# Weight sums begun in the first attention; the second block's head products in plain order, rotary tables loaded wide, x rows' work pinned in program order

## The chip, the cores and the metric

One core of one Trainium2 chip runs the whole program in one launch. The metric is device microseconds of one execution. The kernel before takes 2484.66 us, the median of 3 runs (2481.41 to 2484.78).

## The reference

One layer of a decoder trunk over 2048 tokens of width 1024, all in float32: retention heads beside a pooling mixer behind one combined projection, then cross-attention to 256 memory tokens, then a gated feed-forward with a causal convolution. Cut to what matters:

```
proj = rmsnorm(x) @ w_in                       # 1024 -> 2560: q, k, v, gate (512 each), u (512)
y_ret = silu(g) * head_rmsnorm(retention(rope(q), rope(k), v))     # 4 heads of 128, chunks of 128
y_pool = pool_mixer(u)                         # 4 groups of 128, trailing windows 2, 4, 8, 16
x = x + concat(y_ret, y_pool) @ w_out
s = (rmsnorm(x) @ wq) @ k_mem^T / 16           # 4 heads of 256, 256 memory tokens
x = x + (softmax(s) @ v_mem) @ wo
a = rmsnorm(x) @ w_up                          # 1024 -> 2 * 2816
x = x + (silu(gate(conv3(a))) * val(conv3(a))) @ w_down
return rmsnorm(x)
```

## The kernel before

**Tiling.** The tokens are worked in two blocks b of 1024, each in two halves of 512. A tensor of 1024 x 1024 is eight row tiles k of 128 partitions. Every operand of a product is split into a high and a low part (`split`: ScalarE makes the high part, L258 or with a scale L261; VectorE subtracts it, L242 or L250), and every product is three matmuls, high by high, high by low, low by high (`passes`, L266 to L268), of 128 x 512 each.

**Stages in order of program.** Folding of the weights of memory and cross-attention; block 0: values, head inputs, retention and pooling, output projection with residual; `attention` of block 0; the product of its probabilities with the folded values (tables VWd, with the residual Xd loaded and stored, and the x rows of the next block loaded by `fetch_x`, L578, into T, and split by `load_x`, L261); block 1: `values` and beside it `quarter_sums`, then `head_projections`, output projection, attention, the same product; then the feed-forward over both blocks.

**`attention`** loads the folded memory tables from Md (`load_m`, L927: raw tiles R and S, split into Z at L258), makes the row statistics by small matmuls (L347) of a sum T which VectorE accumulates at L242, and then goes through 16 score tiles: a product, maximum, Exp (L969), division, and two tiles later a transposition (`turn`, L942 and L944).

**`head_projections`** (second block only) makes the sixteen head groups (q 0 to 3, k 4 to 7, gates 8 to 11, pooling groups 12 to 15) in eight pairs, `PAIRS`. For each pair seven products of half the size replace eight: sums of quarters of the weights (Ad, made ahead in DRAM; loaded into R at L1108 and split at L1114) against sums of quarters of x (made by `quarter_sums` and `turned_sums`). `Heads.evac` takes a product out of its accumulator, on ScalarE at L1691 when it is the first of its part, and `Heads.final` finishes a part: rotation for q and k (L1699, L1707), Silu for gates (L1718), negation for pooling groups, which then go through `pool_steps`, a list of VectorE steps. Products 0, 2, 4 and 6 of a pair stand behind one another in pairs 1 to 7 and 1, 3, 5 come after; the first pair has 0 to 6. `settle` splits a finished part for the output projection (E<-Z). Retention of a head (`kept`, L793 to L845) runs piece by piece between the products.

**`weight_sums`** makes the sums of weight quarters in DRAM, on POOL's queue (GpSimd), by DMAs that copy or accumulate: 42 jobs (8 for `PAIRS`, then the feed-forward's) of 8 DMAs in four steps. Each turn of its loop starts one job, and steps all that are live. A turn has a **tick**: a small copy on ScalarE that is kept in program order (L1027, halo<-consts), and behind it a copy on POOL (L1028), after which the DMAs of the turn are issued. Its holder `under[0]` is stepped by other loops, `spacing[0]` of their steps for one turn: by `units` in the output projection and the product after the attention when `slow[0]` is off, by each score tile i of the attention (from i = 2 on in block 0) and by each product of the heads.

**What sets the order.** The program is written as generators which are stepped beside each other. A scheduler that simulates time then moves instructions on each engine within their dependencies; those under `tc.keep_in_program_order` keep their written order among themselves, and `tc.issue_after` holds a DMA behind an instruction. Each engine then takes its instructions strictly in that order, so one that waits holds all behind it.

## Time and profile before

| | |
|---|---|
| median of 3 runs | 2484.66 us |
| the profiled execution's own time | 2485.51 us |
| its span in the trace | 2483.7 us |
| mean granted TensorE clock | 0.991 |
| TensorE busy | 2422.2 us (98%), 11294 matmuls |
| VectorE busy | 1731.1 us (70%) |
| ScalarE busy | 1289.8 us (52%) |
| GpSimd (POOL) busy | 318.8 us (13%) |
| moved by DMA | 501.56 MB |

Where the stages lie in that trace: the first block's output projection runs from about 370 us, its attention's tables are split up to 489, its scores begin at 491, the product of probabilities and values runs to about 664, the second block's values and quarter sums follow up to 705, the heads up to about 940, and the second attention takes in 1000 to 1060.

In the rows of the profile T, R, S, Z, Q, G, E are places in the on-chip memory, mm and aux are accumulators of TensorE, and names that end in d are in DRAM. The arrow in brackets at the end of a timeline row tells how long its engine had stood idle and what released it. "PEclk" is the granted clock of TensorE as a share of the full one. "DMA to landing" gives, for the loads of a line, the least, median and greatest time from issue to landing.

### The profile page before, as it was taken

The page shows a single profiled execution, that of the slowest core. Times are in us where ns is not written, and L with a number is a line of the kernel's source. Part 1 is how long each engine was busy: PE and PEld are TensorE (multiplying, and loading weights), DVE is VectorE, ACT ScalarE, POOL GpSimd, SP SyncE. Part 2 cuts the span into 40 slices and gives each one's busy share as a digit, 9 for nine tenths or more (in the row PEclk, how much of TensorE's full clock was granted, in tenths as well). Part 3 has the DMA queues.
Part 4 walks back from the last instruction along what each step waited for, and adds up shares of the span by engine and source line. Part 5 has one row for each costly group of instructions (what it writes and reads, how often), then busy time and mean ns, then how long its engine had stood idle before and what let it go on. Part 6 is the DMA issues. An engine that isn't in the chain of part 4 may idle for free.

```text
span 2483.7 us, 33285 instructions
## 1 busy us (share of the span) xinstructions
PE 2422.2 (98%) x11294; PEld 2020.2 (81%) x11294; DVE 1731.1 (70%) x2921; ACT 1289.8 (52%) x2348; POOL 318.8 (13%) x485
## 2 busy tenths in 40 slices
PE   6999999899999999999999999999999999999997
PEld 6888888788877787888888888888888888888886
DVE  8646566465665666575688776897667688867876
ACT  6333423343434554434555555665555677666663
POOL 1000003241155544000000000020000000000000
PEclk9999999999999999999999999999999999999998
DMA  8133528977599999557468655665456468768951
GB/s 290 46 108 111 162 73 237 279 173 234 171 296 257 262 235 278 159 175 253 153 187 276 215 187 169 211 219 172 162 157 216 132 223 305 244 189 267 353 173 68
DMA packets 263163, 501.56 MB, mean 202 GB/s; under 512 B 28752, under 2 KB 57552, under 8 KB 262992
## 3 DMA queue, kind: packets, MB, share of 16 engines
q1 hardware_dynamic: 201104, 385.11, 47.3%
q0 software_dynamic: 37376, 86.00, 14.9%
q10 hardware_dynamic: 24512, 28.32, 3.3%
q8 instruction: 89, 1.46, 0.2%
q14 instruction: 82, 0.67, 0.1%
HBM read 398.13 MB, written 187.17 MB: 236 GB/s over the span
## 4 chain that ended last, share of the span: by engine, by line
PE 91%; DMA 4%; DVE 3%; ACT 1%; issue 1%; SPq 0%; POOL 0%; POOLq 0%; ACTq 0%; DVEq 0%
PE mm L266 28%; PE mm L267 28%; PE mm L268 28%; DMA T<-Xd 1%; DMA Z<-xT 1%; PE aux L793 1%; PE aux L804 1%; DMA S<-Md 1%; PE aux L820 1%; PE aux L266 1%; PE aux L267 1%; PE aux L268 1%; DVE Z L242 1%; PE aux L822 1%; DVE T L242 0%
## 5 line engine op out<-in xcount | busy, mean ns | idle before, releaser
L266 PE MATMUL mm<-G,Q 128*128 128x512 f32 (+1 forms) x1745 | 673.6, 387 | 23.0 <-ACT Q L258 10.4
L268 PE MATMUL mm<-G,Q 128*128 128x512 f32 (+1 forms) x1745 | 669.7, 385 | 6.5 <-DVE Q L242 6.3
L267 PE MATMUL mm<-G,Q 128*128 128x512 f32 (+1 forms) x1617 | 620.1, 384 | 0.0
L267 PE MATMUL mm<-G,E 128*128 128x512 f32 x1084 | 421.6, 389 | 0.0
L266 PE MATMUL mm<-G,E 128*128 128x512 f32 x1084 | 420.1, 389 | 0.0
L268 PE MATMUL mm<-G,E 128*128 128x512 f32 x1084 | 419.2, 389 | 0.0
L266 PEld LDWEIGHTS mm<-G,Q 128*128 128x128 f32 x1745 | 331.5, 190 | 89.5 <-ACT Q L258 11.5
L268 PEld LDWEIGHTS mm<-G,Q 128*128 128x128 f32 x1745 | 330.9, 190 | 71.7 <-DVE Q L242 8.8
L267 PEld LDWEIGHTS mm<-G,Q 128*128 128x128 f32 x1617 | 307.5, 190 | 56.3
L242 DVE TENSOR_TENSOR Z<-Z,mm 128x512 f32<-128x512 f32 x296 | 201.8, 683 | 106.4 <-PE mm L268 106.1
L250 DVE SCALAR_TENSOR_TENSOR Z<-Z,vecs 128x1024 f32<-128x1024 f32 x176 | 224.7, 1280 | 50.0 <-ACT Z L1177 46.5
L268 PEld LDWEIGHTS mm<-G,E 128*128 128x128 f32 x1084 | 203.5, 188 | 42.4
L267 PEld LDWEIGHTS mm<-G,E 128*128 128x128 f32 x1084 | 203.5, 188 | 42.2
L266 PEld LDWEIGHTS mm<-G,E 128*128 128x128 f32 x1084 | 203.5, 188 | 42.2
L1114 ACT ACTIVATE E<-R 128x512 fp32r<-128x512 f32 (+1 forms) x165 | 101.5, 615 | 142.0 <-PE mm L267 134.1
L242 DVE TENSOR_TENSOR T<-T 128x512 f32<-128x512 f32 (+3 forms) x220 | 150.9, 689 | 24.2 <-ACT T L409 15.4
L242 DVE TENSOR_TENSOR Q<-R,Q 128x512 fp32r<-128x512 f32 x149 | 103.6, 698 | 71.4 <-ACT Q L258 45.8
L242 DVE TENSOR_TENSOR G<-T,G 128x512 fp32r<-128x512 f32 (+1 forms) x181 | 119.5, 676 | 45.1 <-ACT G L1063 34.8
L1114 ACT ACTIVATE Q<-R 128x512 fp32r<-128x512 f32 (+1 forms) x153 | 94.5, 618 | 94.0 <-PE mm L267 75.0
L1177 ACT ACTIVATE Z<-Z,vecs 128x1024 f32<-128x1024 f32 x88 | 109.2, 1242 | 35.6 <-DVE Z L242 34.6
L1063 ACT ACTIVATE G<-T 128x512 fp32r<-128x512 f32 x157 | 95.7, 624 | 61.0 <-DMA T<-Gd 29.7
L1114 ACT ACTIVATE E<-S 128x512 fp32r<-128x512 f32 (+1 forms) x107 | 65.9, 616 | 106.2 <-PE mm L267 102.7
(337 smaller groups left out, 3799.6 us busy)
## 6 DMA issues: line engine op xcount, KB each, us to landing
T<-Gd SPq DMA_DIRECT2D x168, 256.0 KB, 4.5
Ud<-w_up POOLq DMA_DIRECT2D x132, 256.0 KB, 9.1
Gd<-Z SPq DMA_DIRECT2D x110, 256.0 KB, 2.8
R<-Ud SPq DMA_DIRECT2D x106, 256.0 KB, 2.8
R<-w_up SPq DMA_DIRECT2D x80, 256.0 KB, 3.1
S<-Ud SPq DMA_DIRECT2D x70, 256.0 KB, 2.9
Gd<-T SPq DMA_DIRECT2D x56, 256.0 KB, 3.4
T<-Xd SPq DMA_DIRECT2D x53, 256.0 KB, 4.4
```

The lines of the kernel that those rows point to most:

```text
L242: return eng.tensor_tensor(out=out, in0=a, in1=b, op=op)
L250: dve.scalar_tensor_tensor(out=out, in0=a, scalar=s, in1=b, op0=op0, op1=op1)
L266: pe.matmul(ps, lh, rh, start=start, stop=False, skip_group_check=more)
L267: pe.matmul(ps, lh, rl, start=False, stop=False, skip_group_check=more)
L268: latest[0] = pe.matmul(ps, ll, rh, start=False, stop=stop, skip_group_check=more)
L793: pe.matmul(col(sc, c), self.ch(k, c), self.ch(q, c), start=True, stop=True)
L804: pe.matmul(col(self.kv, c), col(self.kn.f, c), self.ch(v, c, h * T), start=True, stop=True)
L820: pe.matmul(col(y, c), col(self.pr.f, c), self.ch(v, c, h * T), start=True, stop=self.cur[c] is None)
L822: pe.matmul(col(y, c), self.ch(q, c), self.cur[c], start=False, stop=True)
L1063: act.activation(hi, x, AF.Copy)
L1114: act.activation(p2[:, 0, :w], self.raw[i].f[:, :w], AF.Copy)
L1177: act.activation(self.c[g].f, a[:, 2:], AF.Identity, bias=cb[:, f : f + 1], scale=cw[2][:, f : f + 1])
```

## The change

It has six edits. (1) The last pair of `PAIRS` is turned round. (2) The rotary tables in DRAM, `rope_d`, get a third part, the negated sine, made by one ScalarE operation and stored by one more DMA. (3) A flag `paced` lets `units` step the weight sums only after it is set, just ahead of the first attention; in that attention the steps begin with score tile 4 in the place of 2, and each makes a turn (`spacing` 1 in the place of 2). (4) In `quarter_sums` the scaling of one x row by ScalarE and the subtraction of two by VectorE are kept in program order. (5) `head_projections` loads the rotary tables to all 128 partitions by four DMAs and multiplies them by the row norm in four operations, in the place of two loads of 64 partitions and eight operations (`rope_scale`). (6) Products 0 to 6 of every pair come in order, and a pooling group's steps start when both its halves are done, in whichever order.

```diff
-PAIRS = ((15, 8), (0, 4), (14, 9), (1, 5), (10, 11), (2, 6), (3, 7), (12, 13))
+PAIRS = ((15, 8), (0, 4), (14, 9), (1, 5), (10, 11), (2, 6), (3, 7), (13, 12))
...
-    rope_d = drp.tile([2, P, SUB], F32, tag="rope_d", name="rope_d")
+    rope_d = drp.tile([3, P, SUB], F32, tag="rope_d", name="rope_d")
...
-    quarter, slow, spacing = [0], [True], [4]
+    quarter, slow, spacing, paced = [0], [True], [4], [False]
...
-                    if not slow[0]:
+                    if not slow[0] and paced[0]:
                         next(under[0], None)
...
-            if pace > 1 or i > 1:
+            if pace > 1 or i > 3:
                 next(under[0], None)
...
-            act.activation(t, x12, AF.Identity, scale=g1)
-            tt(dve, x12, x11, x12, ALU.subtract)
+            tc.keep_in_program_order(act.activation(t, x12, AF.Identity, scale=g1))
+            tc.keep_in_program_order(tt(dve, x12, x11, x12, ALU.subtract))
...
         def scaled_tables():
-            tables.append(rope_scale(tabs, rb))
+            out = Z.take(2)
+            tables.append(out)
+            for to, half in ((0, 0), (0, 1), (2, 0), (1, 1)):
+                p, i = slice(64 * half, 64 * half + 64), min(to, 1)
+                sp.dma_start(out.f[p, i * T : (i + 1) * T].rearrange("p (s c) -> p s c", s=NS), rope_d[to].rearrange("(s p) c -> p s c", s=NS))
             yield
+            yield
+            for i in range(2):
+                for s in range(NS):
+                    d = out.f[:, i * T + s * SUB : i * T + (s + 1) * SUB]
+                    tt(dve, d, d, rb[s].f[:, :SUB], ALU.mult)
+                yield
...
-                    if q == NS - 1:
+                    self.ended.append(n)
+                    if self.ended.count(n) == NS:
                         todo.append(pool_steps(h, outs[n]))
...
-        items = [(m, i) for m in members for i in (range(7) if m is members[0] else (0, 2, 4, 6, 1, 3, 5))]
+        items = [(m, i) for m in members for i in range(7)]
...
-            for i, r in enumerate(got):
+            minus = TT.take()
+            act.activation(minus.f[:, :SUB], got[1].f[:, :SUB], AF.Copy, scale=-1.0)
+            for i, r in enumerate((*got, minus)):
                 sp.dma_start(rope_d[i], r.f[:, :SUB])
                 r.free()
...
-        spacing[0] = (2, 2)[b]
+        paced[0], spacing[0] = True, (1, 2)[b]
```

The lines of the changed kernel stand 10 to 12 further down from `head_projections` on: L1691, L1718 and L1823 are L1702, L1729 and L1835 there.

**ScalarE, from the first output projection into the attention.** G<-T and T<-T split and square rows of the residual, Xd<-T stores them, Q<-R and Z<-R split weights and memory tables; halo<-consts is the tick. Before, within the output projection:

```order
L258 ACTIVATE G<-T 128x512
L906 DMA Xd<-T 128x512
L409 ACTIVATE T<-T 128x512
L258 ACTIVATE Q<-R 128x512
L1027 ACTIVATE halo<-consts 128x2
L258 ACTIVATE G<-T 128x512
L906 DMA Xd<-T 128x512
L409 ACTIVATE T<-T 128x512
```

Now, from the end of the output projection into the attention's Exps:

```order
L258 ACTIVATE G<-T 128x512
L906 DMA Xd<-T 128x512
L409 ACTIVATE T<-T 128x512
L969 ACT_TABLE_LOAD
L969 ACTIVATE T,sm_3707<-mm_3654,sm_3706,scl_3631 128x256 x2
L969 ACTIVATE T,sm_3746<-mm_3720,sm_3745,scl_3631 128x256 x2
L969 ACTIVATE T,sm_3785<-mm_3759,sm_3784,scl_3631 128x256 x2
L944 ACTIVATE G<-aux_3793 128x4x128
L944 ACTIVATE G<-aux_3839 128x4x128
L969 ACTIVATE T,sm_3831<-mm_3805,sm_3830,scl_3631 128x256 x2
L944 ACTIVATE G<-aux_3885 128x4x128
L1027 ACTIVATE halo<-consts 128x2
```

The eight ticks among the output projection's rows are gone, and the first tick stands behind the attention's fourth Exp. Up to the heads there are twelve in the attention and the product after it; over the whole program there are 45 ticks in both kernels.

**VectorE, in the second block's values and quarter sums.** sm289 to sm291 are the steps that make the reciprocal norms rn287, Q<-consts multiplies them out for TensorE's broadcast (L398), and R_76<-R_76 is the subtraction of two x rows. Before:

```order
L242 TENSOR_TENSOR sm291_5190<-sm290_5188 128x8
L250 SCALAR_TENSOR_TENSOR sm291_5190<-sm291_5190,sm289_5187 128x8
L242 TENSOR_TENSOR R_76<-R_76 128x512
L250 SCALAR_TENSOR_TENSOR sm290_5188<-sm291_5190,sm290_5188 128x8
L1823 COPY rn287_5177<-sm290_5188 128x8
L384 CAST yh292_5218<-rn287_5177 128x8
L242 TENSOR_TENSOR sm293_5219<-rn287_5177,yh292_5218 128x8
L242 TENSOR_TENSOR Q_77<-consts_81,yh292_5218 128x512 x2
```

Now, first the end of the first chain of norms, with an operation of the quarter sums on another row (Z266<-S3) among its steps:

```order
L250 SCALAR_TENSOR_TENSOR sm291_5162<-sm291_5162,sm289_5159 128x8
L250 SCALAR_TENSOR_TENSOR Z266_4490<-S3_79,vecs_80,T_75 128x512
L250 SCALAR_TENSOR_TENSOR sm290_5160<-sm291_5162,sm290_5160 128x8
L250 SCALAR_TENSOR_TENSOR S2_78<-S2_78,vecs_80,Z266_4490 128x512
L250 SCALAR_TENSOR_TENSOR G_72<-S2_78,vecs_80,G_72 128x512
L242 TENSOR_TENSOR sm291_5162<-sm290_5160 128x8
```

and some twenty rows later the subtraction, behind the end of the second chain too (rn298, the norms of the other half):

```order
L250 SCALAR_TENSOR_TENSOR sm302_5280<-sm302_5280,sm300_5277 128x8
L250 SCALAR_TENSOR_TENSOR sm301_5278<-sm302_5280,sm301_5278 128x8
L1835 COPY rn298_5267<-sm301_5278 128x8
L359 CAST yh437_8176<-rn298_5267 128x8
L242 TENSOR_TENSOR R_76<-R_76 128x512
```

The subtraction of the x rows moved behind both chains of norms.

**ScalarE, in the middle of the heads.** S308 and Q_77 are two places for split weights (L1114), out of raw loads R_76 and S3_79. Before:

```order
L1114 ACTIVATE S308_5514<-R_76 128x512
L1691 ACTIVATE Z266_4518<-mm312_5704 128x512
L1114 ACTIVATE Q_77<-R_76 128x512
L1718 ACT_TABLE_LOAD
L1718 ACTIVATE T_75<-T_75 128x512
L1114 ACTIVATE S308_5514<-R_76 128x512
L1027 ACTIVATE halo_94<-consts_81 128x2
```

Now:

```order
L1114 ACTIVATE S308_5484<-R_76 128x512
L1702 ACTIVATE Z266_4490<-mm312_5666 128x512
L1114 ACTIVATE Q_77<-R_76 128x512
L1114 ACTIVATE Q_77<-S3_79 128x512
L1702 ACTIVATE Z266_4490<-mm312_5666 128x512
L1729 ACT_TABLE_LOAD
L1729 ACTIVATE T_75<-T_75 128x512
L1114 ACTIVATE Q_77<-R_76 128x512
L1729 ACTIVATE T_75<-T_75 128x512
L1114 ACTIVATE Q_77<-S3_79 128x512
L1027 ACTIVATE halo_94<-consts_81 128x2
L1702 ACTIVATE Z266_4490<-mm313_5688 128x512
L1114 ACTIVATE S308_5484<-R_76 128x512
```

Between two splits into S308 there was one into Q_77; now there are four. At the end of the heads, on TensorE, 24 matmuls of the output projection that stood behind the last product of retention (L822) stand ahead of it.

More of the change, by code (lines that the diff above doesn't have):

```diff
@@ L1593, in negated, with head_projections @@
         stt(lo, src, -1.0, hi.bitcast(F32), ALU.mult, ALU.subtract)
-    def head_projections(b, v, rb, tabs, t1, t2, z):
+    def head_projections(b, v, rb, t1, t2, z):
         nonlocal raws, prs
@@ L1666, in __init__ @@
                 self.groups, self.how, self.seen, self.acc = PAIRS[p], [""] * 7, set(), None
+                self.ended = []
             def begun(self):
@@ L1942, in trunk @@
             rb = normed[1]
-            tabs = [TT.take() for _ in range(2)]
-            for i in range(2):
-                sp.dma_start(tabs[i].f[:, :SUB], rope_d[i])
-            mix = head_projections(b, v, rb, tabs, t1, t2, z)
+            mix = head_projections(b, v, rb, t1, t2, z)
         for r in rb:
```

## The prediction

> **What bounds the kernel now.** I read the page's chain of waits first, then the busy times by stretch, then TensorE's waits in the stretches where it is not full, and last the timeline around each of these waits.
>
> ```profile
> span 2483.7 us, 33285 instructions
> PE 91%; DMA 4%; DVE 3%; ACT 1%; issue 1%; SPq 0%; POOL 0%; POOLq 0%; ACTq 0%; DVEq 0%
> ```
>
> The first row is the span of the profiled execution, whose own time is 2485.51 us; the median of the three runs is 2484.66. The second row says that TensorE (PE) carries 91% of the chain. The change leaves the number of matmuls alone, so it can only win or lose at the places where TensorE stands still or runs at a lower clock.
>
> ```profile
> core 0: us, PE busy (x) PEld busy (x) DVE busy (x) ACT busy (x) POOL busy (x), PEclk, DMA share, GB/s
> 470.00:500.00 30.00, 21.66 (x87) 17.41 (x86) 16.03 (x39) 7.58 (x14) 3.34 (x6) 0.83 0.74 232
> 580.00:620.00 40.00, 40.00 (x181) 33.05 (x180) 18.88 (x30) 14.51 (x25) 0.00 (x0) 1.00 0.70 245
> 620.00:664.00 44.00, 44.00 (x196) 36.45 (x195) 27.73 (x43) 22.44 (x38) 0.00 (x0) 1.00 0.48 156
> 664.00:700.00 36.00, 31.60 (x146) 26.31 (x145) 25.34 (x55) 12.22 (x23) 15.45 (x25) 0.91 0.89 259
> 750.00:760.00 10.00, 7.93 (x27) 6.22 (x28) 3.85 (x7) 3.60 (x8) 2.20 (x4) 0.83 1.09 294
> 1060.00:1120.00 60.00, 58.19 (x276) 47.74 (x275) 43.34 (x92) 19.77 (x53) 0.00 (x0) 1.00 0.57 188
> ...
> PE aux L347 <- DVE T L242: 7.3, 1, 7.3
> ...
> PE aux L398 <- DVE Q L242: 4.4, 1, 4.4
> ...
> PE mm L266 <- ACT Q L1114: 4.2, 2, 3.3
> ...
> PE mm L266 <- ACT Z L1691: 2.2, 2, 1.3
> PE mm L266 <- ACT Q L1114: 1.8, 3, 0.8
> ```
>
> The last five rows are TensorE's waits in 466 to 500, 660 to 700, 740 to 770 and (two rows) 755 to 950 us: what waited, for what, total, times, longest. Up to the second attention these are its holes: **A**, 7.3 us in the first attention; **B**, 4.4 us where the second block's values and quarter sums begin; **C**, 4.2 us in the head projections, and behind it 4 us in crumbs. The clock column shows what a hole costs beyond itself: 0.83, 0.91 and 0.83 in the stretches of A, B and C, and 1.00 in the two rows between, where TensorE is full.
>
> **Why A is there, and what the later sums do.** The change starts the weight sums in the first attention and no longer in the output projection ahead of it.
>
> ```profile
> 480.27 1.16 ACT L258 ACTIVATE Z<-R 128x512 fp32r<-128x512 f32 x2 [6.21 <-DMA R<-Md]
> 486.45 0.63 ACT L258 ACTIVATE Z<-S 128x512 fp32r<-128x512 f32 x1 [1.28 <-DMA S<-Md]
> 488.93 0.69 DVE L242 TENSOR_TENSOR T<-T 128x512 f32<-128x512 f32 x1
> 489.67 1.86 PE L347 MATMUL aux<-consts,T 128*128 128x1 f32 x8 [7.26 <-DVE T L242]
> 491.39 0.77 PE L267 MATMUL mm<-G 128*128 128x512 f32 x1
> 497.38 0.39 PE L266 MATMUL mm<-G 128*128 128x512 f32 x1
> ...
> DMA to landing us min/median/max: 9.4/11.7/14.1
> ...
> DMA to landing us min/median/max: 4.0/4.5/5.3
> ```
>
> TensorE's statistics matmul waits for VectorE's last row sum (488.93), which stands in VectorE's order behind the low parts of the memory tables, and these stand behind ScalarE's high parts, which wait 6.21 and 1.28 us for the loads of Md. These loads took 11.7 us (the landing row of L927 in 428 to 473, with the weight sums' transfers running); the same loads in the second attention, 1005 to 1025, after the last sum, took 4.5. With the new order the first tick stands behind the fourth tile's Exp of the attention, and Exps begin only after these statistics. So the loads of hole A run without sums: I take 4.5 us for them, 7.2 less than now, and the waits of 6.21 + 1.28 = 7.5 us in front of VectorE's row sum go almost wholly. Gain: 7.3 us of standing. Behind it 14 matmuls, from 491.39 to 497.38, took 5.99 us where the full stretch makes one in 40.00 / 181 = 0.22, that is 3.1: another 2.9. Together 10.2. Low end 8 (something of the wait stays, since 4.5 isn't nothing), high end 7.3 + 0.17 × 30 = 12.4, if all of that row's clock loss is due to the hole. **A: −10.**
>
> The Trainium skill, page "TensorE: Matmul & The Clock Gate", section "Part 1: The HAM clock gate", says that the clock halves once TensorE was idle for a free-running window of about 3.4 us, and comes back after as long a busy one. The trace agrees: holes of 7.3, 4.4 and 3.3 us have clock rows under 1, the stretch 1060 to 1120 with 1.8 us of standing has 1.00; by that rule a hole's aftermath costs 1.7 us or more in the place of my 2.9.
>
> **What the moved sums meet next.** The eight ticks ahead of the attention move into it, so the transfers come later.
>
> ```profile
> 513.26 0.60 ACT L944 ACTIVATE G<-aux 128x512 fp32r<-128x512 f32 x1 [2.82 <-PE aux L942]
> ...
> L1012 POOL DMA_DIRECT2D Ad<-w_qkgu x28 | 17.6, 893 | 2.3 <-DMA Ad<-w_qkgu 2.3
> L1009 POOL DMA_DIRECT2D Ad<-w_qkgu x13 | 11.0, 915 | 13.1 <-DMA Ad<-w_qkgu 12.2 <-issue 0.9
> L1009 POOL DMA_DIRECT2D Ad<-Ad x11 | 9.3, 870 | 16.7 <-DMA Ad<-Ad 12.6 <-DMA Ad<-w_qkgu 4.0
> ...
> DMA to landing us min/median/max: 2.6/9.5/13.4
> ...
> DMA to landing us min/median/max: 2.7/2.8/4.5
> 600.81 3.05 SPq L578 DMA_DIRECT2D T<-xT  x2
> 611.66 3.05 SPq L578 DMA_DIRECT2D T<-xT  x2
> 617.25 0.72 ACT L261 ACTIVATE G<-T,vecs 128x512 fp32r<-128x512 f32 x1 [1.59 <-DMA T<-xT]
> 619.27 0.69 DVE L242 TENSOR_TENSOR Q<-R,Q 128x512 fp32r<-128x512 f32 x1
> 628.39 0.39 PE L266 MATMUL mm<-G,Q 128*128 128x512 f32 x1
> ```
>
> In 370 to 470 POOL spent (17.6 + 2.3 + 11.0 + 13.1 + 9.3 + 16.7) / 52 = 1.35 us on a sum's DMA, waits included. Twelve ticks in the new attention and the product behind it release 4 + 6 + 7 + 9 × 8 = 89 DMAs: 89 us at one a microsecond, 120 at 1.35. The first of them stands behind the third transposed tile, 513.26 on the old clock, so the queue empties between 602 and 633, where the POOL column now shows 0.00 from 580 on. What stands there is the product of the probabilities with the projected values, and its partners are the next block's loads T<-xT: 2.8 us without sums (L578 in 596 to 650), 9.5 and up to 13.4 with them (385 to 465). On ScalarE the split of such a load (617.25) stands ahead of the split of the weights, whose low part is ready at 619.96 and first used at 628.39: 8.4 us of cover. A unit takes 611.66 − 600.81 = 10.85 us; the loop from one load to the next is the landing plus about 6 us (the load's second half is issued 2.7 later, then three ScalarE operations of 0.6 to 0.7, a VectorE one of 0.69 and the issue). So landings up to 4.9 us cost nothing, and one of 9.5 costs 4.6 a unit. Up to 3 units fall between 601 and 633: 3 × 4.6 − 8.4 = 5.4 at most; nothing, if the queue is empty by 610. I take **+2**, with 0 and +10 as ends (+10: two of the three at 13.4 us).
>
> Later the ticks run until about 1020 in the place of 1000, and the last loads of Md in the second attention, at 4.5 us now, may meet a few sums: 0 to +8 (hole A over again), and I take **+1**. No instruction is lost or gained otherwise but the one that negates the sine table, and its store, in the attention: 0.7 us of ScalarE, which was under 8 us busy in the 30 of its row; nothing. The head tables are now four multiplications of 128 partitions (0.69 each by the L242 rows) in the place of eight on 64, behind four loads which are two yields early: nothing, if the loads land under about 12 us, as those of 11.7 do.
>
> **Program order for the x rows (B).**
>
> ```profile
> 687.82 0.72 ACT L1577 ACTIVATE T<-R,vecs 128x512 f32<-128x512 f32 x1 [9.36 <-DMA R<-xT]
> 688.57 0.69 DVE L242 TENSOR_TENSOR R<-R 128x512 f32<-128x512 f32 x1 [5.83 <-ACT T L1577]
> ```
>
> VectorE's subtraction of two x rows (688.57) was put in the midst of the chain that makes the reciprocal norms; it waits 5.83 us for a row from DRAM, the last three operations of the chain wait behind it, and then TensorE's broadcast (L398). In the new order the subtraction comes behind the whole chain, and L398 stands 10 matmuls, 2.3 us, later. But another quarter-sum operation on a late row (Z<-S) now stands ahead of the chain's end; its load is issued about 6 us earlier than now, so a wait of 0 to 2 us may stay. Gain 4.4 plus 1.7 of clock (half of the shortfall 0.09 × 36 = 3.2), less the rest: −4 to −6.7. **B: −5.5.**
>
> **Products 0 to 6 in order (C).**
>
> ```profile
> 748.88 0.63 ACT L1114 ACTIVATE S<-R 128x512 fp32r<-128x512 f32 x1 [5.10 <-DMA R<-Ad]
> 751.40 0.61 ACT L1114 ACTIVATE Q<-S 128x512 fp32r<-128x512 f32 x1
> ...
> 914.63 0.69 DVE L242 TENSOR_TENSOR Z<-Z,mm 128x512 f32<-128x512 f32 x1 [0.70 <-PE mm L268]
> 927.54 0.39 PE L822 MATMUL aux<-T,E 128*128 128x128 f32 x2
> 945.39 0.63 ACT L258 ACTIVATE E<-Z 128x512 fp32r<-128x512 f32 x1
> ```
>
> In C ScalarE waits 5.10 us for the load of an operand that it needs later, ahead of the one that TensorE waits for (751.40). In the new order four other splits stand between the two of that kind, so the hole (4.2, plus 0.17 × 10 = 1.7 of clock) should go; and with 0, 1, 2, 3 in turn the products of one bank no longer follow each other, which takes up to 2.2 + 1.8 of the crumbs. That is −6 to −10 within the heads. It is handed back at their end: the last operand of the output projection (E<-Z, ready at 945.39 + 0.63) comes 18.5 us after TensorE's last retention product (927.54), through a chain of pooling and normalising on VectorE and ScalarE that the change does not shorten. TensorE has some 15 us of work to set against it now; in the new order 24 of these matmuls (5.4 us) are already done before that product, so a wait of 18.5 − 10.3 = 8 us, less what is there now (1.3 of it at E), is new: +6 to +8. **C: −2**, between −6 and +3.
>
> **The sum.** −10 + 2 + 1 − 5.5 − 2 = −14.5: 2471.0 in the profiled execution's terms, and with the median 0.85 below it, 2470.
>
> **The rivals.**
>
> First, *the moved sums choke the stage after the attention*, which ends on the slower side. It needs POOL's queue to last until 640 and T<-xT to land as slowly as the worst do now (13.4). Then a unit takes 8.5 us longer than 10.85, four to four and a half units are hit, and past the 8.4 us of cover TensorE stands 4.5 × 8.5 − 8.4 = 30 us: 2471 − 2 + 30, less the clock it keeps, about 2495. For it: the DMA share is already 0.70 in 580 to 620 without any sum, and POOL's own pace fits an end near 633. Against it: DMA falls to 0.48 from 620 on, and the median landing is 9.5, not 13.4. It decides from the point where sums last beyond three units with landings over 9 us. The Trainium skill, page "DMA: Bandwidth & Descriptors", section "Queues, rings and completion order", says that each DMA engine goes round the queues that have work for it, packet by packet; by it SP's loads share with POOL's sums wherever both are queued, so A's loss would move and not vanish. The landing rows, 9.5 against 2.8, agree with that.
>
> Second, *hole A moves into the second attention*: sums last past 1010, its loads of Md take 11.7 us, and 7 to 10 us come back: about 2480. Against it: only the last three of these loads are near the end of the sums.
>
> Third, *the heads give back all and more*: the tail wait is 8 us with its clock (+3), and B keeps its 2 us: −10 + 2 + 1 − 4 + 5 = −6, about 2479.
>
> Fourth, *A does not hang on the sums*: the attention's loads of Md take 11 us because of the loads T<-xT and Z beside them. Then A stays and the rest gives −4: about 2481. The 4.5 us of the second attention, which has other company, is all that speaks against it.
>
> **How the numbers follow.** A measurement of this kernel can tell 0.2%, 5 us, from no change: faster is under 2479.7, slower over 2489.6. The forecast has 0.62 (its own range, from the terms' ends with not all at once at their best or worst, 2461 to 2480), the first rival 0.16, the second 0.08, the third 0.09, the fourth 0.05. The range reaches from 2460 to 2485, which leaves out most of the first rival and the tips of the others. Faster: 0.60 of the forecast, 0.04, 0.06 and 0.02 of the second to fourth: 0.72. Slower: 0.13 of the first, 0.02 of the forecast, 0.01 of the fourth: 0.16. The rest, 0.12, is the same.
>
> **What would show it.** A is right if L347's wait is under 1 us and the loads of Md before it land in about 4.5; if they land slowly and no sum runs, the fourth rival holds. The first rival shows as TensorE's waits for the weights Q in 600 to 660 with T<-xT over 5 us. B shows as L398 waiting under 2 us. C shows as no wait for L1114's splits over 1 us, and a wait of 5 to 8 us for E near the end of the heads; no such wait means my tail term is wrong and the time is nearer to 2464. From the tenth score tile of the second attention on all engines but POOL have the same order, so both executions should run that part equally long; if they don't, something outside this account is at work.

## The result: no change that can be told, and the profile after

The changed kernel takes 2485.08 us (median of 12 runs, 2478.80 to 2489.05), the kernel before beside it 2484.09 us (median of 12). The ratio is 1.0001, with a 95% interval of 0.9991 to 1.0011. The forecast was 2470 us, so it was wrong, although the hole that it started from is gone. The profiled execution of the changed kernel took 2483.87 us, with a span of 2482.1.

TensorE's waits of the changed kernel from 370 to 1130 us, as the view of waits gives them (what waited, for what, total, times, longest):

```profile
PE aux L942 <- DVE T L246: 12.5, 4, 4.2
PE mm L268 <- DVE Q L242: 6.9, 3, 2.6
PE aux L398 <- DVE Q L242: 2.4, 1, 2.4
PE mm L266 <- ACT E L258: 1.9, 1, 1.9
PE aux L845 <- ACT T L840: 0.6, 1, 0.6
PE mm L266 <- ACT Q L258: 0.5, 1, 0.5
PE aux L266 <- DVE E L250: 0.3, 1, 0.3
```

L347's 7.3 us and L1114's 4.2 have no row any more. In their place stands a wait that the prediction did not name, 12.5 us of L942: the transposition of a tile of probabilities, which waits for VectorE's division. Next the stretches, with the columns of the same view of before:

```profile
470.00:500.00 30.00, 30.00 (x145) 25.05 (x144) 21.25 (x57) 12.32 (x29) 0.00 (x0) 1.00 0.36 127
500.00:580.00 80.00, 76.20 (x360) 62.30 (x358) 40.43 (x95) 32.76 (x84) 43.34 (x71) 1.00 0.91 224
580.00:620.00 40.00, 36.27 (x156) 30.15 (x157) 17.99 (x30) 14.43 (x26) 13.67 (x23) 0.96 1.05 348
664.00:700.00 36.00, 33.56 (x157) 27.85 (x156) 27.31 (x66) 14.81 (x27) 17.59 (x26) 0.95 0.93 265
900.00:960.00 60.00, 52.40 (x262) 42.43 (x261) 36.58 (x79) 22.45 (x59) 30.34 (x44) 0.97 0.90 238
1000.00:1060.00 60.00, 56.36 (x269) 46.52 (x268) 32.19 (x82) 21.23 (x51) 10.90 (x15) 1.00 0.67 170
```

The first row is full now, at full clock and without sums. In the next two TensorE lost 3.8 and 3.7 us where it was full before, and so it did at 1000 to 1060.

Both programs have 11294 matmuls, and the change only moves them locally. So the start of the n-th matmul, set against that of before, tells where time went. This table does that for the changed kernel and for the experiments below, in us from the start of the span; each column is one profiled execution, and the steps from row to row are what counts.

| n | before at | change | e1 | e2 | e3 | e8 | e12 | f1 | f2 | f3 |
|---|---|---|---|---|---|---|---|---|---|---|
| 2300 | 452.49 | +1.2 | +0.0 | +0.3 | +0.3 | −0.4 | −1.5 | −0.3 | −0.9 | +1.6 |
| 2500 | 507.62 | −11.2 | −2.3 | −12.1 | −12.1 | −12.8 | −13.9 | −12.7 | −13.3 | −10.8 |
| 2700 | 550.08 | −7.7 | −2.3 | −12.1 | −12.1 | −12.8 | −13.9 | −12.7 | −5.7 | −10.8 |
| 2900 | 592.57 | −2.0 | −2.3 | −12.1 | −12.1 | −12.8 | −13.9 | −12.5 | −2.9 | −10.8 |
| 3400 | 709.13 | −4.6 | −8.4 | −7.0 | −15.5 | −17.6 | −15.6 | −18.9 | −6.5 | −13.0 |
| 4500 | 935.75 | −14.0 | −16.7 | −6.0 | −23.7 | −21.9 | −26.6 | −25.1 | −15.8 | −23.4 |
| 4600 | 961.46 | −7.0 | −9.7 | −4.8 | −17.7 | −18.0 | −23.0 | −17.9 | −9.1 | −15.6 |
| 4800 | 1006.79 | −7.0 | −9.7 | −4.8 | −17.6 | −18.0 | −22.9 | −17.9 | −9.1 | −15.1 |
| 5000 | 1048.97 | −2.9 | −9.6 | +1.2 | −11.5 | −17.9 | −22.7 | −17.0 | −5.3 | −11.6 |
| 11293 | 2473.13 | −1.4 | −9.1 | −0.6 | −13.0 | −19.0 | −24.4 | −7.9 | −7.0 | −11.4 |

The column of the change reads: −12.4 at hole A; **+9.2 in the rest of the first attention** (2500 to 2900); nothing in the stage behind it, where the prediction looked for the sums' harm; −2.6 at B; −9.4 within the heads; +7.0 at their end; **+4.1 in the second attention**. The two in bold make most of what the prediction missed.

What is waited for shows in the chain of waits of the changed kernel, cut to the first attention (start, length, what):

```profile
521.16 7.45 DMA rope_d<-T
528.63 8.86 DMA T<-xT
537.51 0.63 ACT T L405
538.13 0.49 ACT G L944
538.71 1.10 ACT T L969 x4
540.04 0.36 DVE T L246
540.54 0.63 PE aux L942 x4
...
566.16 6.92 DMA rope_d<-T
573.16 7.48 DMA T<-xT
580.67 0.72 ACT G L261
```

Read it from below upward. TensorE's L942 needs the division (L246), that needs Exp (L969), and Exp stands in ScalarE's order behind the square of an x row (L405), whose load could be issued only when the store of a rotary table had given back a T place. The second time it is the store of the negated sine, at 566.16, and TensorE goes on at 583.73. The four x loads of this stretch are issued at 521.6, 528.6, 566.6 and 573.2 here. Store and load are slow as the weight sums run: in 495 to 600 us the loads T<-xT (L578) land, before and after, as

```profile
DMA to landing us min/median/max: 2.8/4.6/7.7
...
DMA to landing us min/median/max: 7.5/8.9/11.9
```

In the second attention the rows of the changed kernel's timeline are

```profile
1017.18 1.15 ACT L258 ACTIVATE Z<-S 128x512 fp32r<-128x512 f32 x2 [5.55 <-DMA S<-Md]
1023.72 1.16 ACT L258 ACTIVATE Z<-S 128x512 fp32r<-128x512 f32 x2 [5.39 <-DMA S<-Md]
1032.24 0.70 PE L942 MATMUL aux<-consts,T 128*128 128x128 f32 x4 [3.64 <-DVE T L246]
1033.88 0.82 POOL L1009 DMA_DIRECT2D Dd<-Dd  x1 [0.48 <-DMA Dd<-Dd]
```

The last sum is issued at 1033.88 in the place of 1004.08 before, and the last load of Md, issued at 1007.97, took 15.7 us in the place of 4.0. The first attention has the reverse: the loads of Md in 428 to 473 landed in 9.4/11.7/14.1 us before, and after in

```profile
DMA to landing us min/median/max: 3.5/3.6/5.7
```

### The profile page after: what moved, and what is told of

It is laid out like the page before. It is cut to its first block, busy times and chain, and to the rows that moved or that the text cites. A ratio compares the mean times of both kernels' runs of the same rounds, so it can differ in the third digit from the quotient of the medians.

```text
span 2482.1 us, 33252 instructions
## 1 busy us (share of the span) xinstructions
PE 2418.8 (97%) x11294; PEld 2018.0 (81%) x11294; DVE 1726.2 (70%) x2917; ACT 1290.9 (52%) x2349; POOL 319.5 (13%) x485
## 4 chain that ended last, share of the span: by engine, by line
PE 87%; DMA 6%; DVE 4%; ACT 1%; issue 1%; SPq 0%; POOLq 0%; POOL 0%; DVEq 0%; ACTq 0%
PE mm L268 27%; PE mm L266 27%; PE mm L267 27%; DMA T<-xT 2%; DVE Z L242 1%; DMA S<-Md 1%; DVE G L242 1%; DMA rope_d<-T 1%; PE aux L820 1%; PE aux L793 1%; PE aux L804 1%; DVE T L242 1%; PE aux L266 1%; DVE Q L242 1%; PE aux L267 1%
## 5 line engine op out<-in xcount | busy, mean ns | idle before, releaser
L266 PE MATMUL mm<-G,Q 128*128 128x512 f32 (+1 forms) x1745 | 672.3, 386 | 17.3 <-ACT Q L258 11.5
L268 PE MATMUL mm<-G,Q 128*128 128x512 f32 (+1 forms) x1745 | 668.7, 385 | 13.3 <-DVE Q L242 13.2
L1114 ACT ACTIVATE E<-R 128x512 fp32r<-128x512 f32 (+1 forms) x165 | 101.5, 615 | 141.0 <-PE mm L267 132.1
L242 DVE TENSOR_TENSOR T<-T 128x512 f32<-128x512 f32 (+3 forms) x220 | 150.6, 690 | 21.3 <-ACT T L409 12.5
L1114 ACT ACTIVATE Q<-R 128x512 fp32r<-128x512 f32 (+1 forms) x153 | 94.6, 618 | 87.1 <-PE mm L267 70.9
L1114 ACT ACTIVATE E<-S 128x512 fp32r<-128x512 f32 (+1 forms) x107 | 65.8, 615 | 104.9 <-PE mm L267 101.3
## 6 DMA issues: line engine op xcount, KB each, us to landing
Ud<-w_up POOLq DMA_DIRECT2D x132, 256.0 KB, 10.3
```

Of the source, the lines that this page charges most:

```text
L242: return eng.tensor_tensor(out=out, in0=a, in1=b, op=op)
L266: pe.matmul(ps, lh, rh, start=start, stop=False, skip_group_check=more)
L268: latest[0] = pe.matmul(ps, ll, rh, start=False, stop=stop, skip_group_check=more)
L1114: act.activation(p2[:, 0, :w], self.raw[i].f[:, :w], AF.Copy)
```

## The experiments

Each kernel was run in five rounds beside the kernel before. A ratio is that to the kernel before on the same chip.

**e1: the pacing undone.** Theory S, the sums; theory M, the third store.

```diff
-                    if not slow[0] and paced[0]:
+                    if not slow[0]:
-            if pace > 1 or i > 3:
+            if pace > 1 or i > 1:
-        paced[0], spacing[0] = True, (1, 2)[b]
+        spacing[0] = (2, 2)[b]
```

> The change with its pacing of the weight sums undone (sums begin in the output projection again, two steps to a turn). In the profile of the change the 7.3 us hole at L347 is gone, but three waits of TensorE for transposable probabilities (L942) are new: 3.3 us at 540, 4.2 us at 584 in the first attention and 3.6 us at 1032 in the second. Theory S: these three come from the weight sums, which now run densest beside the first attention's x loads and rope stores and end later. Then here L347 waits about 7 us again, L942 waits under 1.5 us at all three places, and the time is 12.4 - 9.2 - 4.0 = -0.8 against the change: 2482 to 2486. Theory M: the two in the first attention come from the third rope store, which keeps a T place from the x loads. Then L347 waits 7 us and L942 still waits 3 to 8 us in the first attention: 2488 to 2494.

Measured 2475.60 us, ratio 0.9965 (0.9952 to 0.9979). Its waits from 470 to 600:

```profile
PE aux L347 <- DVE T L242: 6.0, 1, 6.0
PE mm L267 <- DVE Q L242: 0.2, 1, 0.2
```

The waits are those of theory S: L347 is back and L942 has none in the first attention; in the second it waits 1.7 us, as in the kernel before (1.8). But the time is below both ranges and 9 us below the change, so the new pacing, as part of this change, loses more than it wins.

**e2: the pacing alone**, in the kernel before (the edits of e1 the other way).

> The kernel before with the new pacing alone. Theory S: the L347 hole goes (-12), but L942 waits 5 to 9 us in the first attention and 3 to 4 us in the second: 2480 to 2486, no change against before that can be told. Theory M: the L347 hole goes, no L942 wait over 1.5 us in the first attention, 4 in the second: -8, 2474 to 2478.

Measured 2484.57 us, ratio 1.0007 (0.9998 to 1.0015). The time is in S's range, but not for its reason: the view of waits has no row at all from 470 to 600. The gain of 12.4 is given back at L398 (9.4 us in the place of 4.4, for the unpinned subtraction waits longer beside the later sums) and in the second attention (+6). So both theories were half right: without the third store the first attention keeps its gain.

**e3: two stores**, the sign put on in the multiplication.

```diff
-            for to, half in ((0, 0), (0, 1), (2, 0), (1, 1)):
+            for to, half in ((0, 0), (0, 1), (1, 0), (1, 1)):
...
-                    tt(dve, d, d, rb[s].f[:, :SUB], ALU.mult)
+                    if i == 0:
+                        tt(dve, d, d, rb[s].f[:, :SUB], ALU.mult)
+                    else:
+                        stt(d[:64], d[:64], -1.0, rb[s].f[:64, :SUB], ALU.mult, ALU.mult)
+                        tt(dve, d[64:], d[64:], rb[s].f[64:, :SUB], ALU.mult)
...
-            minus = TT.take()
-            act.activation(minus.f[:, :SUB], got[1].f[:, :SUB], AF.Copy, scale=-1.0)
-            for i, r in enumerate((*got, minus)):
+            for i, r in enumerate(got):
```

> The change with no negated sine stored: rope_d has two parts again, the head tables are still loaded wide, and the sign is put on by the multiplication (64 partitions each for the sine table). Theory M: the x loads get their T places early again, both L942 waits in the first attention fall under 1.5 us, and the time falls by 6 to 9 us to 2476 to 2479. Theory S: the waits stay at 6 us or more together and the time stays within 3 us of the change, 2482 to 2488.

Measured 2472.55 us, ratio 0.9957 (0.9944 to 0.9969): 12.5 us below the change by the medians and 11 by the ratios, more than theory M's 6 to 9. No wait in 470 to 600. Its four x loads are issued at 505.0, 520.7, 521.4 and 528.2. Its ScalarE has the two squares apart, with Exps between them, while the changed kernel has them side by side (two rows of e3's timeline, then two of the change's):

```profile
509.60 0.63 ACT L405 ACTIVATE T<-T 128x512 f32<-128x512 f32 x1 [1.80 <-DMA T<-xT]
530.59 0.63 ACT L405 ACTIVATE T<-T 128x512 f32<-128x512 f32 x1 [7.27 <-DMA T<-xT]
```

```profile
530.62 0.63 ACT L405 ACTIVATE T<-T 128x512 f32<-128x512 f32 x1 [6.39 <-DMA T<-xT]
537.51 0.63 ACT L405 ACTIVATE T<-T 128x512 f32<-128x512 f32 x1 [6.26 <-DMA T<-xT]
```

**e4: the old order of products**, and of the last pair, in the change.

> The change with the old order of products (0, 2, 4, 6, 1, 3, 5 from the second pair on) and the last pair (12, 13). By the theory that the new order wins 9.5 us within the heads (750 to 935) and gives 7.1 us back behind the last retention product: the wait of 3.3 us for L1114 near 750 and the crumbs are back, the waits for E and Q between 925 and 955 fall from 7 us to about 2.5, and the time is +2.4: 2485 to 2490. Rival: the end of the heads is late for another cause (the pooling chain is as late as here with any order); then the heads lose 9.5 and the end keeps its 7 us: 2492 to 2497.

Measured 2490.16 us, ratio 1.0029 (1.0017 to 1.0040), just above the range of the first theory: the new order is worth 5 us here by the medians and 7 by the ratios. The wait for L1114 near 750 (2.9 us) is back and the give-back behind the heads is +1.1 in the place of +7.0.

**e5: old pacing and two stores** together.

> The change with the pacing undone and two stores (no negated sine stored) at once. e1 and e3 each won about 9 to 13 us against the change. Theory of an interaction: the third store costs only where the sums run beside it densely; with the old pacing there was no L942 wait in the first attention to take away, so this is e1's time, 2473 to 2478, with L347 waiting 5 to 7 us and no L942 wait over 1.5 us there. Rival, two costs that add: 2475.6 - 12.5 = 2463, 2460 to 2466.

Measured 2474.99 us, ratio 0.9970 (0.9959 to 0.9981), as e1: the two do not add. The third store costs nothing beside the old pacing.

**e6: sums two tiles earlier**, in e3.

```diff
-            if pace > 1 or i > 3:
+            if pace > 1 or i > 1:
```

> e3 (two stores) with the weight sums begun at score tile 2 of the first attention in the place of 4, one turn a tile: two turns earlier, so that the two ticks that now fall into the second attention would come before it. Theory: the L942 wait of 3.1 us at 1021 and the 6 us between the 4800th and the 5000th matmul come from sums that still run there; they go by half or more (loads of Md land in under 8 us), 2466 to 2471. Rival: the queue of sums is held up by the transfers themselves, not by its start, and ends as late as in e3: 2471 to 2475. A hole at L347 over 3 us would show that the sums now reach back to the first loads of Md.

Measured 2478.26 us, ratio 0.9979 (0.9970 to 0.9988), above both ranges and slower than e3. Its profiled execution, the fastest of its 12 runs (2469.8), ends the sums earlier, as was meant: the last one is issued at 992, the last load of Md lands in 4.3 us, and L942 waits 1.0 us in the place of 4.1. But the stretch from the 4800th to the 5000th matmul still costs 5.9 us. The hole has moved ahead of the statistics, where ScalarE now waits 6.7 and 4.6 us for two earlier loads of Md, issued at 978.76 and 993.26 and landed in 10.1 and 6.0 us. The second of these waits, and TensorE behind it:

```profile
999.27 0.63 ACT L258 ACTIVATE Z<-R 128x512 fp32r<-128x512 f32 x1 [4.55 <-DMA R<-Md]
1000.99 1.22 PE L266 MATMUL mm<-G 128*128 128x512 f32 x2 [2.31 <-ACT G L258]
```

The split that TensorE waits for (G) stands on ScalarE behind the one that waits for that load. The theory's sign, quick last loads, came; its gain did not. What the longer of the runs wait for was not seen.

**e7: pins off**, in e3.

> e3 without the two pins in quarter_sums. Theory: the subtraction of two x rows goes back into the chain of norms, and with the sums running there L398 waits as in e2 (9.4 us) in the place of 3.1: plus 5 to 9 us, 2477 to 2482. Rival: the pins are worth nothing, L398's wait follows the sums alone: 2470 to 2475.

Measured 2472.83 us, ratio 0.9966 (0.9954 to 0.9978): not to be told from e3. L398 waits 8.4 us in the place of 3.1, as the theory said, but the hole at 720 that e3 has behind it (2.7 us, explained under e12) is gone in return, the start of its program is 1.7 us shorter, and at the end 0.6 us are left.

**e8: the last pair in the old order**, in e3.

```diff
-        items = [(m, i) for m in members for i in range(7)]
+        items = [(m, i) for m in members for i in (range(7) if m is not members[-1] else (0, 2, 4, 6, 1, 3, 5))]
```

> e3 with the products of the last pair alone in the old order (0, 2, 4, 6, 1, 3, 5). Theory of the tail: what TensorE gives back between the 4500th and the 4600th matmul (6 to 7 us) is the wait for E and Q behind the last retention product, because 24 matmuls less stand there; with the last pair in the old order 60 matmuls stand between that product and E in the place of 42, 18 x 0.23 = 4.1 us more cover: the give-back falls by 4 to 6 us, 2466 to 2470. Rival: the pooling of the last groups is then later by as much: 2471 to 2475.

Measured 2466.77 us, ratio 0.9945 (0.9931 to 0.9959); the interval overlaps that of e3, so 3 us by the ratios and 6 by the medians are not clear of noise. The give-back behind the heads falls only from 6.1 to 3.9. The rest comes where nobody looked: the second attention costs nothing (4800 to 5000). Two things differ there. By the order, 53 matmuls stand between the statistics and the first transposition in the place of 47, 1.4 us more; and ScalarE gets the last load of Md 4.8 us after the statistics begin (1011.51 after 1006.74) in the place of 7.2 (1012.49 after 1005.25). Neither was tried alone.

**e9, e10, e11: the pins alone, the products alone, the tables alone**, each in the kernel before.

> The kernel before with the two pins in quarter_sums alone. The prediction's term B: L398's wait falls from 4.4 to under 1 us and the clock there rises: -5.5, 2476 to 2479. Rival, after e7 where the pins won 6 us up to the 3400th matmul and had 0 left at the end: what is won is waited for at the next load (the hole at 750, where the next weight sum has to land), 2481 to 2484.

> The kernel before with the products in order 0 to 6 and the last pair turned, alone. The prediction's term C: the hole of 3.3 us at L1114 and the crumbs of 750 to 935 go (-9), 6 to 7 us come back behind the last retention product: -2 to -3, 2479 to 2482. Rival, after e4: in the change the same edit is worth 5 us, since nothing else moved there: 2476 to 2479.

> The kernel before with the rotary tables' edits alone (third store of the negated sine, wide loads, four multiplications). Theory: with the old pacing the third store costs TensorE nothing (no L942 wait over 1.5 us in the first attention), and the wide loads leave a wait of 2.5 to 3.5 us for VectorE's low parts near 727 (Q, L242), which may be swallowed by the hole at 750: 2482 to 2487. Rival: the third store alone costs as in the change: 2490 to 2494.

Measured 2478.26 us, 0.9988 (0.9979 to 0.9997); 2476.07 us, 0.9976 (0.9966 to 0.9986); 2480.07 us, 0.9996 (0.9987 to 1.0005), beside 2481.51 of the kernel before. The pins won 2.7 us at L398 (2.2 us of waiting are left), half of term B: the time lies in the first theory's range only because the kernel before was at 2481.51 here. The products win 5.4, more than term C. The tables are worth nothing there, third store and all; the time is below both ranges. The three ratios together make 0.9960; e1, which has all three, has 0.9965. Within their intervals they add; the pacing does not add to them.

**e12: e8 with the narrow tables** of the kernel before (`rope_scale`, two loads).

> The change with two stores, the narrow tables of the kernel before (rope_scale), and the old order of products in the last pair alone: e8 without the wide loads. Theory: the wait of 3.5 us for Q at 719 in e8 (VectorE stands behind the four loads of the wide tables) goes, the rest stays: 2462 to 2466. Rival: behind that hole stands a load that comes no earlier, so nothing is won: 2466 to 2469.

Measured 2461.65 us (median of 4), ratio 0.9922 (0.9908 to 0.9935): **the fastest of all, 0.8% below the kernel before**, and just under the first range. The wait that it takes away, in the changed kernel's timeline of VectorE and TensorE:

```profile
726.58 1.29 DVE L242 TENSOR_TENSOR Z<-Z,T 128x512 f32<-128x512 f32 x2 [7.54 <-DMA Z<-rope_d]
728.37 1.29 DVE L242 TENSOR_TENSOR Z<-Z,T 128x512 f32<-128x512 f32 x2 [0.50 <-DMA Z<-rope_d]
729.58 0.69 DVE L242 TENSOR_TENSOR Q<-R,Q 128x512 fp32r<-128x512 f32 x1
730.92 0.50 PE L268 MATMUL mm<-G,Q 128*128 128x512 f32 x1 [2.63 <-DVE Q L242]
```

The multiplications of the wide tables wait for their loads, and the low part of a weight operand, ready to be made, stands behind them. What e12 still waits for from 370 to 1130:

```profile
PE mm L266 <- ACT Q L258: 4.9, 2, 4.4
PE aux L398 <- DVE Q L242: 3.1, 1, 3.1
PE mm L266 <- ACT Q L1114: 1.1, 1, 1.1
PE aux L942 <- DVE T L246: 0.4, 1, 0.4
```

Three more runs were to settle which part of the third store it is, and which part of the pacing.

**f1: half the density**, in the change.

```diff
-        paced[0], spacing[0] = True, (1, 2)[b]
+        paced[0], spacing[0] = True, (2, 2)[b]
```

> The change with spacing 2 in the first attention in the place of 1 (a turn of the weight sums every second score tile, from tile 4 on). Theory of density: with gaps between the turns the x loads land in 3 to 5 us now and then, as in e1, and the two L942 waits of the first attention fall from 7.5 us to under 3; the sums end later still and the second attention waits 3 to 6 us: 2478 to 2484. Rival, the place alone decides: the two waits stay at 6 us or more: 2485 to 2492.

Measured 2475.17 us, ratio 0.9976 (0.9967 to 0.9986), below the range of the density theory. No wait in 470 to 600, with all three stores; the loads T<-xT landed there in 2.6 to 7.9 us, in the change in 7.5 to 11.9. The sums run on to 1082, and from 1000 to 1120 there are waits of

```profile
PE aux L942 <- DVE T L246: 8.8, 5, 2.6
```

All but 0.5 us of them stand behind 1060, in the later tiles of the second attention: the 8.5 us that f1 loses again lie between the 5200th and the 5350th matmul.

**f2: the place without the store**, in e3; **f3: the store without the place**, in e3.

```diff
+            minus = TT.take()
+            act.activation(minus.f[:, :SUB], got[1].f[:, :SUB], AF.Copy, scale=-1.0)
             for i, r in enumerate(got):
                 sp.dma_start(rope_d[i], r.f[:, :SUB])
                 r.free()
+            minus.free()
```

```diff
                 sp.dma_start(rope_d[i], r.f[:, :SUB])
+                if i:
+                    sp.dma_start(rope_d[2], r.f[:, :SUB])
                 r.free()
```

> e3 (two stores) with the negated sine still made into a T place of its own, which is given back at once and not stored (nothing reads it). Theory of the place: the x loads of the first attention get their T places as late as in the change, two squares (L405) stand side by side on ScalarE again, and L942 waits 3 to 8 us in the first attention: 2478 to 2485. Theory of the transfer: no L942 wait over 1.5 us there: 2470 to 2475.

> e3 with a third store all the same: the sine table is stored twice from its one place (nothing reads the second copy). Theory of the place: as e3, no L942 wait over 1.5 us in the first attention, 2470 to 2475. Theory of the transfer: L942 waits 3 to 8 us there, 2478 to 2485.

Measured 2476.18 us, 0.9975 (0.9966 to 0.9984), and 2473.49 us, 0.9963 (0.9949 to 0.9977). f3 has no wait in 470 to 600: the transfer as such costs nothing. f2 issues its x loads at 519.5, 527.9, 569.5 and 569.9, much as the change does, has the two squares side by side again, and waits

```profile
PE aux L942 <- DVE T L246: 7.2, 2, 5.8
```

in its profiled execution, 5.8 at the first place and 1.3 at the second, where the change has 3.3 and 4.2. In that execution the place alone costs as much in the first attention as place and store in the change (10.4 and 9.2 us from 2500 to 2900). By all runs it costs less: 3 us (0.9975 against f3's 0.9963, and these intervals overlap), with the store 6.5 more (1.0001, clear of f2). f2's runs lie between 2470.98 and 2481.35, the profiled one, 2478.32, near their upper end; how often the two holes come up in the others was not seen. So beside dense sums the waits come with the place and not without it, and the store adds to them: the second hole, 4.2 us in the place of 1.3, is that place waiting 6.9 us for its store.

## Why the prediction was wrong

**Hole A: right.** The prediction had −10; the step is −12.4 in the pair of profiled executions, the loads of Md landed in 3.6 us in the place of 11.7, and e1 and e2 bring the wait back and take it away with the pacing alone. The execution profiled first had more of it than others: kernels with the old pacing waited 4.3 to 6.0 us at L347, so the typical gain is nearer to 9 or 10.

**What the moved sums meet next: the failed step.** The prediction followed the sums past the attention, into the product of probabilities and values, and took +2 there. Its count of 89 transfers was right, and the last was issued at 635.6, later than the 602 to 633 forecast. But TensorE waits for nothing from 596 to 664, and the reason is not the one given. The first loads T<-xT of the four units landed in 11.9, 9.7, 7.2 and 6.8 us; by the prediction's loop, in which all beyond 4.9 us is lost, that makes 16.0, less the 8.4 of cover 7.6 us. Those loads were issued at 598.8, 609.7, 620.6 and 631.9, about a unit apart: the second left before the first had landed. So landing plus 6 us is not what paces them, and that +2 was nearly right was luck. The prediction did not look into the attention itself, where the sums now run one turn a tile. And it closed the cost of the third store with "0.7 us of ScalarE ... nothing": it counted the instruction, and not the T place that the instruction's result keeps until its store has landed. The place delays an x load, the load delays a square on ScalarE, Exp waits behind the square, and TensorE waits for Exp. Size: 9.2 us in the profiled pair; change against e3 is 11 us by the ratios. It needs both edits: old pacing with three stores (e1, e11), and new pacing with two (e2, e3), have none of it; f1, with all three stores, shows that a lull between turns is enough to be rid of it.

**The second attention: right mechanism, wrong size.** The prediction took +1 of 0 to +8; it was +4.1 in the change and +6 in e2 and e3. It was not one of several small risks: the sums end 30 us later, and a load of Md that took 4.0 us takes 15.7. The second rival named it, at 7 to 10 us, and was given 0.08. What the sums cost there does not follow their end alone: e6 ended them at 992 and lost 5.9 us at earlier loads, while e8 and e12 ran them to 1020 and 1015 and lost nothing.

**B: right mechanism, half the size.** −2.6 in place of −5.5. In e1, where the sums were not moved, the step to 3400 is −6.1, and L398 waits 0.3. In the change a wait of 2.4 stays, which is the 2 us that the prediction held possible and a little more. It is for the late row that the prediction named (Z<-S): its load is issued at 674.1, where e1 issues it at 671.1, and takes about as long (9.5 and 10.1 us). Why it is issued later was not tried; the last load T<-xT ahead of it is later too (658.4 and 656.4). Part of the gain hangs on the wide tables, which was not forecast. e8 and e12 differ by the tables alone: with the narrow ones, whose loads T<-rope_d stand among the x rows on SP's queue, that row takes 12.2 us in the place of 9.5, and L398 waits 3.1 in the place of 1.7. In e9, narrow tables too, it takes 12.3.

**The wide tables: wrong.** "Nothing, if the loads land under about 12 us": they landed in 6.7 to 10.3 and cost 2.6 us of standing, since they were issued as late as 716 to 718, behind loads of weights on SP's queue and after a wait of SP for VectorE of 2.7 us. e8 and e12 differ by these tables alone, and by 5 us, net of what the wide ones win at L398.

**C: right, and larger than forecast.** −9.4 in the heads and +7.0 behind them, where −6 to −10 and +6 to +8 were forecast. The measured net of the edit, 5 to 7 us (e4) and 5.4 (e10), is at the good end of −6 to +3 or just beyond it. The −9.4 holds the loss at the wide tables as well; by itself the edit wins more than forecast within the heads, 12.6 us in e10, 5.4 up to the 3600th matmul and 7.2 behind it, where the prediction counted crumbs of 4.0. The tail's explanation was only in part right. TensorE waits 1.9 us for E there, and 4.3 for the low parts of Q, which the prediction's sign did not name; and 18 matmuls more of cover gave 2.2 us, not 4.1 (e8).

**The sum and the rivals.** With the profiled pair's steps, −12.4 + 9.2 − 2.6 − 9.4 + 7.0 + 4.1 = −4.1, and the start and the end of the program add 1.2 and 1.5. The prediction expected no difference behind the 5000th matmul; these 1.5 us have no account here, and apart from f1 the other columns differ there by −1.8 to +0.5. The first rival had the right cause, sums that move a loss and do not end it, but in the wrong stage; the fourth rival is refuted by the 3.6 us.

By the rule that the Trainium skill gives on its page "DMA: Bandwidth & Descriptors", in "Queues, rings and completion order", a DMA engine goes round the queues that have work for it, packet by packet. The runs agree with such sharing (11.7 and 3.6 us for the same loads with and without sums on POOL's queue), and had the prediction followed it to each load beside the sums, and not to the one stage that it had in view, it would have met the loads of x.

## What to carry to other kernels

Background transfers that are moved away from one wait need a look at every load of the stretch that they move into, those of the same stage first: which place each load is waiting for, and what stands behind its consumer on an in-order engine. A temporary that is stored costs its place until the store has landed; count that time, at the landing times of the new neighbourhood, and not the instruction. And when edits are judged one by one, judge them also in pairs: here three of four add up in the total, and the fourth turns an edit that costs nothing alone into 11 us.

## What the runs showed of the hardware that was not expected

The clock does not follow the length of a hole. In the changed kernel the holes of 3.34 us at 540 and 3.64 us at 1032 left the granted clock at 1.00, and the one of 2.44 us at 689 (L398) brought it down to 0.83, with seven matmuls behind it that start 0.4 to 0.6 us apart in the place of 0.23 (columns as above):

```profile
536.00:546.00 10.00, 6.66 (x32) 5.29 (x31) 5.93 (x15) 6.48 (x20) 6.88 (x13) 1.00 0.68 167
686.00:696.00 10.00, 7.56 (x27) 5.77 (x27) 6.97 (x27) 3.92 (x7) 5.50 (x10) 0.83 1.05 331
1028.00:1038.00 10.00, 6.36 (x32) 4.95 (x31) 6.15 (x22) 5.85 (x16) 2.42 (x4) 1.00 0.80 168
```

So the length of about 3.4 us on which the prediction's sentence about the clock rests does not divide these holes. The work ahead of the hole does not decide it either. The hole at L398 in e6, 2.93 us long and with the same matmuls ahead of it, left the clock at 1.00:

```profile
676.00:686.00 10.00, 8.00 (x35) 6.61 (x36) 7.83 (x28) 5.31 (x10) 6.55 (x11) 1.00 1.06 310
```

It is the same at the hole of the wide tables: behind 2.47 us in e1 eight matmuls start 0.3 to 0.6 us apart, and behind 3.16 us in e6 they are 0.23 us apart again from the second on. So the price of a hole's aftermath, 0 to some 3 us here, can't be told from its length beforehand; what sets it stays open.
